# A two-layer hybrid trunk: finished tiles a stage earlier with rows in freed token space, norms and tables in fixed rounds, casts on ScalarE, the first rotation from PSUM

## Chip, core and metric

The kernel runs on one core of a Trainium2 chip. The metric is the device time of one execution in microseconds (us); before the change the median of 3 runs is 2095.43 us (2093.11 to 2095.86).

## The reference

Two layers over 2048 tokens of width 1024, each `x + y @ w_out`, then a last RMS norm. `y` joins chunked softmax attention (8 heads of 64, own chunk and 8 chunks before, a relative bias) and chunkwise retention (4 heads of 128, rotary phases, a decaying state, a norm per head), both gated with silu:

```python
hn = rms_norm(x, norm_gain)
aq, ak, av, ag, rq, rk, rv, rg = jnp.split(hn @ w_in, cuts, axis=-1)
ya = chunked_rel_attention(aq, ak, av, rel_bias)
yr = chunkwise_retention(rq, rk, rv, cos, sin)
y = jnp.concatenate([ya * silu(ag), yr * silu(rg)], axis=-1)
return x + y @ w_out
```

`rms_norm` is `x * lax.rsqrt(mean(x*x) + EPS)` times the gain. `cos` and `sin` come from `positions` times a table of inverse frequencies, and `apply_rotary` gives `[t1*c - t2*s, t1*s + t2*c]` for the two halves of a head.

## The kernel before

**Precision.** Every large product is made of three float16 products: an operand is split into a float16 upper part and a float16 remainder (`h` and `l` in the names: `hTh`/`hTl` the normed tokens, `wh`/`wl` the weights), and upper x upper, upper x remainder and remainder x upper are summed in PSUM: 24 matmuls for a contraction of 1024. Weights are first scaled by a power of two taken from their sum of squares: a square pass on ScalarE with an accumulator (`sumsq`), a cast of the sum to bfloat16 (`lowp`, on VectorE, line 316), a matmul with ones that sums over partitions (`allsum`, line 323), a few one-column operations (`norm_scale`), then the upper part on ScalarE and the remainder on VectorE (`convert`).

**Stages.** A tile is 128 tokens, a block 512 tokens (4 tiles; n = 0 to 3), a head group s = 0 to 3 is two attention heads and one retention head. For each layer l, group s and block n there are two stages. The T stage (`dense_T`, matmul line 731, output `dT`) makes queries and keys with features on the partitions, in four matmul groups j = 0 to 3 (attention query, attention key, retention query, retention key). The V stage (`dense_V`, line 752, output `dV`) makes values and gates with tokens on the partitions, in four groups a = 0 to 3, one a tile. Each group has 24 matmuls of 512 columns in 3 rounds of 8, so a stage has 12 rounds. Group sums lie in a pool of two PSUM buffers (`psD`); a buffer is free again when ScalarE and then VectorE have taken their parts from it: `v`, `gt`, `rv` on lines 760 to 763, then 766 to 770 one round later.

**Order.** The order on TensorE, ScalarE, VectorE and GpSimd is the order in which the Python code issues; only SyncE, which issues all DMAs, is ordered by a scheduler after the start. `run` drives a stage: after each round it executes what is due in a list of postponed steps (`later(k, fn)`: k rounds on), then one step of the attention of the block before, then some steps of background generators: `push(gen, steps)` queues one, and `run` deals the steps left over the rounds left (its last argument). Attention on a unit (tile a, head hx) is: scores into the one PSUM buffer `S` (lines 800, 801), bias and maximum on VectorE into a tile `sc` (line 804), exponential on ScalarE, probabilities split into `pq` (ScalarE, GpSimd), a DMA transpose to `pT`, and the product with the values (lines 820 to 822). Tiles `sc` and `pq` have two buffers each.

**Start.** The start (layer 0, group 0, block 0) is written out by hand as a list of steps. Tiles 0 to 3 are normed and transposed on TensorE; tiles 4 to 7 (`Tok`) are normed in the first V stage and turned by DMA transposes (lines 236, 237). In that first block the queries and keys of retention are copied from PSUM (`raw`, line 662), their halves are swapped by two DMAs (`swp`, lines 666, 667), and four 128x512 operations follow on VectorE (lines 670, 676). The product of keys and queries for retention's first tile (`decayed`, line 860) comes in the first attention step.

**Norms of blocks 2 and 3 and tables.** `norms_from_input` is a background generator for four tiles: load, square (ScalarE), root (VectorE, GpSimd), multiply (VectorE), upper rows (ScalarE), remainder rows (VectorE), DMA transposes. Its rows lie in the buffers of `sc` and `pq` (`row_pair`). Tables of sine and cosine for a block are 18 steps (`tables`): range reduction on VectorE, two sines on ScalarE (lines 121, 122, each change of function set a table load), eight small stores. Both run as background of the stages of the block before.

**Output projection.** Once the last group is done, `wout` goes over the 16 tiles (line 1105, `dO`). A finished row tile `y` is loaded, squared for its scale, split into rows (`rhy`, `rly`, again in the buffers of `sc` and `pq`), turned by DMA transposes into `yhy`, `yly` (`y_turn`). For the first two tiles `wout_first` does this in the last V stage (s = 3, n = 3), as background. `prep_Omax` sums the squares of `w_out` in eight pieces during the V stage of s = 2, n = 2.

## Time and profile before

| | |
|---|---|
| median of 3 runs | 2095.43 us |
| the profiled execution | 2094.75 us |
| its span on the core | 2092.8 us |
| TensorE busy / VectorE / ScalarE / GpSimd | 2004.4 / 1343.8 / 1141.3 / 432.9 us |
| mean granted TensorE clock | 0.991 |

The span runs from the first to the last instruction. A line of a timeline has the start, the length, the engine, the source line, the operation, its output and inputs by name and the count; in brackets stands the idle time before it and what ended it. A line of the waits has who waited for whom, the total, the count and the longest. Matmuls are pipelined: one that is shown with 0.38 us starts 0.22 us after the one before it at full clock.

### The profile page before, as it was taken

How to read it: one execution, taken by the hardware profiler on the slowest of the kernel's cores; microseconds unless marked ns; L12 is line 12 of the kernel's file. 1: busy time of each engine (PE TensorE's matmuls, PEld its weight loads, DVE VectorE, ACT ScalarE, POOL GpSimd, SP SyncE). 2: the span in 40 equal slices, each digit the busy share in tenths (PEclk: the TensorE clock that was granted, in tenths of full speed). 3: DMA queues.
4: the chain of work that ended last, by engine and by line, in shares of the span. 5: the costliest groups of instructions: out<-in, count | busy, mean ns of one | idle time of the engine just before them, and what ended most of it. 6: DMA issues, size and time to landing. Idle time of an engine off the chain costs nothing.

```text
span 2092.8 us, 39599 instructions
## 1 busy us (share of the span) xinstructions
PE 2004.4 (96%) x14014; PEld 1049.4 (50%) x14014; DVE 1343.8 (64%) x4031; ACT 1141.3 (55%) x2522; POOL 432.9 (21%) x509
## 2 busy tenths in 40 slices
PE   6888999999999999998999999999999999998998
PEld 4344455555555555444444555555555555554443
DVE  7676666666656666576654666666666667656643
ACT  7455665556565654455444546554655565455432
POOL 1022222222122212121000222222222222222100
PEclk9999999999999999999999999999999999999999
DMA  8767674557476764599965556655655776558874
GB/s 247 171 127 162 136 166 114 115 112 159 110 169 133 161 166 99 113 211 260 219 185 113 120 102 142 130 121 106 155 123 118 178 156 162 117 100 183 212 199 123
DMA packets 645702, 313.65 MB, mean 150 GB/s; under 512 B 459232, under 2 KB 602080, under 8 KB 645504
## 3 DMA queue, kind: packets, MB, share of 16 engines
q1 hardware_dynamic: 645504, 311.12, 66.4%
q8 instruction: 110, 1.80, 0.4%
q14 instruction: 88, 0.72, 0.1%
HBM read 123.26 MB, written 41.98 MB: 79 GB/s over the span
## 4 chain that ended last, share of the span: by engine, by line
PE 55%; DMA 7%; DVE 5%; ACT 3%; issue 1%; SPq 1%; POOL 0%; POOLq 0%; DVEq 0%; ACTq 0%
PE dT L731 18%; PE dV L752 15%; PE dO L1105 12%; DMA pT<-pq 2%; PE r L860 2%; PE S L801 2%; PE S L800 2%; PE o L820 1%; PE o L821 1%; PE o L822 1%; DVE sc L804 1%; DMA swp<-rot 1%; DMA yhy<-rhy 1%; ACT sc L807 1%; ACT pq L809 1%
## 5 line engine op out<-in xcount | busy, mean ns | idle before, releaser
L810 POOL TENSOR_TENSOR pq<-sc,pq 128x640 f16<-128x640 f32 (+4 forms) x256 | 323.8, 1265 | 1175.9 <-issue 590.7
L807 ACT ACTIVATE sc<-sc,mq,cT 128x640 f32<-128x640 f32 (+4 forms) x256 | 218.5, 853 | 558.1 <-DVE mq L806 413.7
L752 PE MATMUL dV<-whV,hTh 128*128 128x512 f16 x1024 | 354.5, 382 | 13.0 <-DVE gt L770 12.8
L731 PE MATMUL dT<-hTh,whT 128*128 128x512 f16 x1008 | 349.4, 382 | 14.7 <-DMA hTh<-hTl 9.6
L752 PE MATMUL dV<-wlV,hTh 128*128 128x512 f16 x1024 | 354.1, 381 | 0.0
L752 PE MATMUL dV<-whV,hTl 128*128 128x512 f16 x1024 | 354.0, 381 | 0.0
L731 PE MATMUL dT<-hTl,whT 128*128 128x512 f16 x1008 | 346.6, 379 | 0.0
L731 PE MATMUL dT<-hTh,wlT 128*128 128x512 f16 x1008 | 346.6, 379 | 0.0
L752 PEld LDWEIGHTS <-hTh 128*128 128x128 f16 x2048 | 197.3, 98 | 227.7 <-DVE gt L770 16.4
L731 PEld LDWEIGHTS <-whT 128*128 128x128 f16 x2016 | 192.9, 98 | 221.6 <-issue 24.1
L804 DVE CUSTOM_DVE_ANT_0 sc<-S,bias 128x640 f32<-128x640 f32 (+4 forms) x256 | 188.4, 736 | 78.8 <-PE S L801 61.1
L1105 PE MATMUL dO<-whO,yly 128*128 128x512 f16 x512 | 194.1, 379 | 2.4 <-DMA yly<-rly 2.4
L1105 PE MATMUL dO<-whO,yhy 128*128 128x512 f16 x512 | 194.0, 379 | 1.2 <-DVE gt L770 0.6
L1105 PE MATMUL dO<-wlO,yhy 128*128 128x512 f16 x512 | 194.0, 379 | 0.0
L809 ACT ACTIVATE pq<-sc 128x640 f16<-128x640 f32 (+4 forms) x256 | 171.5, 670 | 10.9 <-DMA pT<-pq 3.0
L1105 PEld LDWEIGHTS <-yhy 128*128 128x128 f16 x1024 | 99.6, 98 | 115.1 <-issue 0.8
L752 PEld LDWEIGHTS <-hTl 128*128 128x128 f16 x1024 | 99.7, 98 | 105.0 <-issue 2.8
L800 PE MATMUL S<-k,q 128*128 128x128 f16 (+3 forms) x592 | 143.1, 268 | 7.9 <-DVE mq L804 7.9
L731 PEld LDWEIGHTS <-wlT 128*128 128x128 f16 x1008 | 97.2, 98 | 101.8 <-issue 1.1
L820 PE MATMUL o<-v,pT 128*128 128x65 f16 x1120 | 129.6, 193 | 10.2 <-DMA pT<-pq 9.7
L801 PE MATMUL S<-k,q 128*128 128x128 f16 (+3 forms) x592 | 130.5, 268 | 0.0
L820 PEld LDWEIGHTS <-pT 128*128 128x128 f16 x1120 | 105.3, 97 | 49.2 <-DMA pT<-pq 21.3
(350 smaller groups left out, 3352.7 us busy)
## 6 DMA issues: line engine op xcount, KB each, us to landing
q<-qq SPq DMA_DIRECT2D x128, 128.0 KB, 2.7
yyy<-y_d SPq DMA_DIRECT2D x32, 512.0 KB, 4.6
stT<-in_w_in_dram SPq DMA_DIRECT2D x27, 512.0 KB, 4.8
stV<-in_w_in_dram SPq DMA_DIRECT2D x26, 512.0 KB, 4.5
k<-kk SPq DMA_DIRECT2D x128, 64.0 KB, 2.0
swp<-rot SPq DMA_DIRECT2D x64, 128.0 KB, 2.5
tabc<-tab SPq DMA_DIRECT2D x32, 256.0 KB, 2.7
tabs<-tab SPq DMA_DIRECT2D x32, 256.0 KB, 2.9
```

The lines of the kernel that those rows point to most:

```text
L731: pe.matmul(ps, w_[:, j, kt, :], h_[:, kt, :], start=(m == 0), stop=(m == 23))
L752: pe.matmul(ps, h_[:, kt, a * P:(a + 1) * P], w_[:, kt, :], start=(m == 0), stop=(m == 23))
L800: pe.matmul(o, st.q[:, hx, 0, cs], k_, start=True, stop=False)
L801: pe.matmul(o, st.q[:, hx, 1, cs], k_, start=False, stop=True)
L804: dve.tensor_tensor_reduce(out=v, in0=S[:, 0:w], in1=g.bias[hx][:, 640 - w:640], scale=1.0, scalar=-3.0e38, op0=ALU.add, op1=ALU.max, accu ...
L807: act.activation(v, v, AF.Exp, bias=m[:, 0:1], scale=g.c[:, 0:1])
L809: act.activation(pq[:, 0:w], v, AF.Copy)
L810: pool.tensor_tensor(pq[:, w:2 * w], v, pq[:, 0:w], op=ALU.subtract)
L820: pe.matmul(o[:, 0:65], u.p[:, b, :], v_[:, 0:65], start=(b == 0), stop=False)
L821: pe.matmul(o[:, 0:64], u.p[:, b, :], v_[:, 65:129], start=False, stop=False)
L860: pe.matmul(out_, w_, m_, start=(i == 0), stop=(i + 1 == len(pairs)))
L1105: pe.matmul(ps, h_[:, kt, :], w_[:, kt, :], start=(m == 0), stop=(m == 23))
```

## The change

- **Finished tiles.** `wout_first` runs from the T stage of s = 3, n = 3 on, a stage earlier, in 16 steps that also turn the second tile. Rows of tiles 0 to 5 (of all tiles in the last layer) and the turned forms of tiles 0 and 1 lie in spaces of normed tokens that are no longer read (`areas`, `quarter`), not in `row_pair` and not in table space.
- **Fixed rounds.** From block 1 on the first group no longer deals background steps. `slot(r, fn)` ties a step to round r, counted from the first V stage: norms of block 2 from round 18 and of block 3 from round 39, one tile every 3 rounds, loads 4 rounds ahead of the square; tables at given rounds; the weights of the next group from round 57. Rows lie in free token or start-up space, inputs in the load pool `w4` of three buffers. Block 1's T stage spans rounds 12 to 23, its V stage 24 to 35, block 2's follow from 36 and 48, block 3's from 60 and 72.
- **Casts.** `lowp` is on ScalarE, and adds two sums there where there are two.
- **First rotation.** In the first block VectorE multiplies straight from PSUM, the sine in two half-partition operations that swap the halves; the copies and swap DMAs of that block go. `decayed` for the first tile comes in the first V stage, at its 11th round.
- **Block 1's first two groups** are computed tile by tile (128 columns at a time, both groups open): 192 matmuls of 128 columns where there were 48 of 512.
- **Output-weight norms** are spread over the T and the V stage of s = 2, n = 2, with loads two pieces ahead and one reduction at the end.

```diff
-    def lowp(m1, nm):
+    def lowp(m1, nm, more=None):
         mb = b2.tile([P, 1], BF16, tag="mb", name=f"mb{nm}", bufs=4)
-        dve.tensor_copy(mb, m1)
+        if more is None:
+            act.activation(mb, m1, AF.Copy)
+        else:
+            act.activation(mb, m1, AF.Identity, bias=more[:, 0:1])
         return mb
...
+        def first_rotation(j, ps, rot):
...
+            def cosine():
+                dve.scalar_tensor_tensor(out=own, in0=ps, scalar=2.0 ** -16, in1=st.tabc, op0=ALU.mult, op1=ALU.mult)
+
+            def sine(half):
+                if half == 0:
+                    st.swp = b1.tile([P, 512], F32, tag="swp", name=f"swp{nm}_{j}")
+                i_, o_ = slice((1 - half) * 64, (2 - half) * 64), slice(half * 64, half * 64 + 64)
+                dve.scalar_tensor_tensor(out=st.swp[o_], in0=ps[i_], scalar=-2.0 ** -16, in1=st.tabs[i_], op0=ALU.mult,
+                                         op1=ALU.mult)
...
+            d = 2 * j
+            later(d, cosine)
+            later(d, lambda: sine(0))
+            later(d + 1, lambda: sine(1))
+            later(d + 2, lambda: dve.tensor_tensor(own, own, st.swp, op=ALU.add))
+            later(d + 3, lambda: act.activation(rot[:, 0], own, AF.Copy))
+            later(d + 4, lambda: dve.tensor_tensor(rot[:, 1], own, rot[:, 0], op=ALU.subtract))
...
+        parts = (l, s, n) == (0, 0, 1)
+        if parts:
+            ps, m = [None] * 2, 0
+            for (j, a) in ((0, 0), (0, 1), (0, 2), (1, 0), (1, 1), (1, 2), (0, 3), (1, 3)):
+                if a == 0:
+                    ps[j] = psD.tile([P, 512], F32, tag="dense", name=f"dT{nm}_{j}")
+                cs = slice(a * P, (a + 1) * P)
+                for i in range(24):
+                    w_, h_ = ((g.h, hh), (g.l, hh), (g.h, hl))[i // KT]
+                    pe.matmul(ps[j][:, cs], w_[:, j, i % KT, :], h_[:, i % KT, cs], start=(i == 0), stop=(i == 23))
...
+    def areas(l):
+
+        if l + 1 == DEPTH:
+            return [hT[l, i] for i in range(3)]
+        return [hT_of(l + 1, i) for i in (NS - 1, 1, 2)]
+
+    def quarter(area, i):
+        return area[i // 4].rearrange("p k c -> p (k c)")[:, i % 4 * D:(i % 4 + 1) * D]
...
-        u.rows = row_pair(u.nm)
+        if u.t < 6 or l + 1 == DEPTH:
+            i = (u.t + 2) % 6 * 2
+            u.rows = [quarter(areas(l)[2 - i // 8], (i + j) % 8 if i < 8 else 4 + (i + j) % 4) for j in range(2)]
+        else:
+            u.rows = row_pair(u.nm)
...
+            for fn in slots.pop(ring["round"], ()):
+                fn()
+            ring["round"] += 1
+            if left is None:
+                continue
...
+            for i, fn in ((-4, load), (0, sq), (1, root), (2, mul), (3, lambda: rows_hi(rows, u.x)),
+                          (4, lambda: rows_lo(rows, u.x)), (5, lambda: transpose_rows(rows, *u.h))):
+                slot(r + i, fn)
...
+    table_steps(t1, (12, 12, 13, 13, 14, 15, 17, 17))
+    table_steps(t2, [18] + list(range(22, 36)) + [36, 38, 38])
+    table_steps(t3, [36] + list(range(40, 54)) + [54, 56, 56])
+    norms_from_input(18, range(8, 12), late[0:4])
+    norms_from_input(39, range(12, 16), xs0[0:2])
+    first_prep = 57
+    for r in range(first_prep, 96):
+        for _ in range((r + 1 - first_prep) * 48 // 39 - (r - first_prep) * 48 // 39):
+            slot(r, lambda: pull(1))
+    slot(first_prep - 1, lambda: push(prep_T(0, 1, grp(0, 1)), 25))
...
+                if n == 2 and s == 2:
+                    push(prep_Omax(l, go), 23)
...
                 if n == NS - 1 and s == NSW - 1:
                     us = []
-                    push(wout_first(l, go, us), 10)
-                if n == 2 and s == 2:
-                    push(prep_Omax(l, go), 13)
+                    push(wout_first(l, go, us), 14)
+                if not first:
+                    run(dT, att, None if (l, s) == (0, 0) or (l, s, n) == (0, 1, 0) else 10 if n == 0 else 24)
```

More of the change, by code (lines that the diff above doesn't have):

```diff
@@ L693, in swap @@
                     else:
-                        later(d + 5 if first else 11, tokens)
+                        later(11, tokens)
                 if j == 2:
@@ L1150, in grp, with slot @@
         return groups[l, s]
+    slots = {}
+    ring["round"] = 0
+    def slot(r, fn):
+        slots.setdefault(r, []).append(fn)
     def run(gen, att, thirds):
@@ L1215, in hybrid_trunk, with table_steps @@
+    def table_steps(gen, rounds_):
+        for r in rounds_:
+            slot(r, lambda: next(gen, None))
     xa = b3.tile([P, 2, D], F32, tag="wh", name="xa")
```

209 lines of the change are left out of this document (111 added, 98 removed).

## The prediction

> **What bounds the kernel now.** I read the page's span first, then busy time in windows cut at the first matmul of each stage, then TensorE's waits, then the time lines round the longest of them.
>
> ```profile
> span 2092.8 us, 39599 instructions
> ```
>
> The profiled execution took 2094.75 us, 1.95 outside its span; the median shown is 0.7 above it. The columns below are the window, its length, and busy time (count) of PE, PEld, DVE, ACT and POOL, then granted clock and DMA.
>
> ```profile
> 48.39:78.91 30.52, 20.88 (x98) 9.30 (x97) 18.59 (x38) 14.56 (x31) 1.90 (x5) 0.88 0.87 195
> 78.91:103.55 24.64, 24.44 (x134) 11.84 (x135) 18.84 (x60) 12.88 (x25) 4.08 (x7) 0.94 0.52 133
> 103.55:140.13 36.58, 27.22 (x161) 12.85 (x159) 27.55 (x77) 22.29 (x50) 6.80 (x11) 0.95 0.68 129
> 140.13:166.03 25.90, 25.90 (x195) 13.82 (x196) 19.28 (x55) 13.12 (x28) 7.70 (x8) 1.00 0.64 118
> 166.03:204.90 38.87, 29.33 (x208) 15.47 (x205) 27.25 (x74) 23.10 (x48) 7.88 (x10) 0.91 0.81 177
> 204.90:236.33 31.43, 28.15 (x203) 14.51 (x204) 17.97 (x63) 18.98 (x39) 7.54 (x7) 0.95 0.69 150
> 236.33:264.20 27.87, 26.30 (x209) 14.51 (x207) 19.65 (x64) 16.50 (x40) 5.87 (x7) 1.00 0.66 128
> ...
> 599.36:627.92 28.56, 26.63 (x208) 14.36 (x206) 16.64 (x60) 20.34 (x47) 5.85 (x7) 1.00 0.87 194
> 654.09:680.23 26.14, 26.14 (x209) 14.43 (x207) 21.01 (x65) 17.20 (x41) 6.79 (x8) 1.00 0.54 114
> 859.50:893.80 34.30, 29.53 (x208) 15.32 (x206) 21.48 (x64) 19.08 (x40) 5.84 (x7) 0.90 0.68 125
> 893.80:945.00 51.20, 47.70 (x360) 25.23 (x361) 36.55 (x105) 29.25 (x54) 13.61 (x13) 1.00 0.92 215
> ...
> 1128.39:1151.17 22.78, 22.78 (x134) 11.39 (x133) 10.65 (x43) 10.81 (x27) 2.99 (x6) 1.00 0.36 84
> 1151.17:1175.72 24.55, 24.55 (x164) 12.46 (x162) 18.43 (x63) 15.88 (x41) 4.08 (x5) 1.00 0.49 119
> 1612.37:1640.74 28.37, 26.55 (x208) 14.36 (x206) 16.63 (x58) 20.22 (x47) 6.29 (x7) 1.00 0.89 197
> 1872.42:1906.64 34.22, 28.31 (x208) 15.03 (x205) 21.49 (x64) 19.08 (x40) 5.84 (x7) 0.95 0.65 138
> ```
>
> TensorE sets the time: a clean full stage is 26.14 us with TensorE never idle. Time beyond that stands in few places: block 0's V stage (30.52), block 1 (24.64 + 36.58, against 22.78 + 24.55 for the same work in layer 1: 13.9 over), block 2 (25.90 + 38.87: 12.5 over two clean stages), block 3 (31.43 + 27.87: 7.0 over), the two stages with the output-weight norms (28.56, 28.37: 4.7 over) and each layer's last V stage (34.30, 34.22: 16.2 over). These are the stages that the change edits. What TensorE waits for there:
>
> ```profile
> PE dV L752 <- DVE gt L770: 12.8, 6, 4.9
> PE dT L731 <- DMA hTh<-hTl: 9.6, 1, 9.6
> ...
> PE msT L323 <- DVE mbT L316: 3.3, 3, 1.9
> ...
> PE msV L323 <- DVE ya L832: 2.9, 2, 1.6
> ```
>
> ```profile
> 48.39 1.89 PE L752 MATMUL dV<-whV,hTh 128*128 128x512 f16 x8
> 50.11 1.89 PE L752 MATMUL dV<-whV,hTl 128*128 128x512 f16 x8
> ...
> 78.91 3.26 PE L731 MATMUL dT<-hTh,whT 128*128 128x512 f16 x8 [9.64 <-DMA hTh<-hTl]
> ...
> 192.54 0.61 PE L752 MATMUL dV<-whV,hTh 128*128 128x512 f16 x1 [4.25 <-DVE gt L770]
> ...
> 204.90 1.44 PE L731 MATMUL dT<-hTh,whT 128*128 128x512 f16 x3 [2.81 <-DMA hTh<-rhn]
> ...
> 878.17 0.27 PE L800 MATMUL S<-k,q 128*128 128x128 f16 x1 [3.28 <-DVE mq L804]
> ```
>
> The reader is to see three kinds of wait: for transposed tokens that land late (9.64, 2.81), for a PSUM buffer that ScalarE and VectorE empty late (4.25), and for attention scores that VectorE has not taken (3.28). A long one costs more than itself: the eight matmuls after 9.64 us took 3.26 us where eight take 1.89, and the three after 2.81 us took 1.44. The Trainium skill ("TensorE: Matmul & The Clock Gate", Part 1) has the clock fall to half only after about 3.4 us of idleness; by it nothing would be won back behind the waits of 2.81 and 3.28 us, and with an estimate of 2 us for each of them and for layer 1's like of the second my sum would be 6 us higher, near 2058. The 2.81 us row shows the slowing all the same, so the measurement decides and the sum stands.
>
> **Block 0's V stage, with the first rotation.** The late landing comes from SyncE's queue, where three 512 KB loads of later tiles and the swap copies stand before the last transposes:
>
> ```profile
> 70.71 0.57 SPq L1171 DMA_DIRECT2D hTh<-in_x_dram  x1
> ...
> 73.10 1.53 SPq L236 DMA_TRANSPOSE hTh<-hTl  x1
> 74.73 2.92 SPq L237 DMA_TRANSPOSE hTl<-hTl  x1
> ```
>
> Afterwards those loads go into later rounds, the four swap copies are gone, and block 1's T stage starts with tile 4 alone. That removes 9.64 and the slowing, 3.26 - 1.89: 11.0 in all. The price is on VectorE:
>
> ```profile
> 37.45 0.68 DVE L634 SCALAR_TENSOR_TENSOR qq<-dT,qq 128x512 f16<-128x512 f32 x1
> ...
> 62.77 0.28 DVE L766 SCALAR_TENSOR_TENSOR v<-dV,v 128x128 f16<-128x128 f32 x1
> ```
>
> A 512-wide operation from PSUM is 0.68. Each rotation now takes five (cosine, two half-sines, sum, remainder), and both fall in this stage: ten, 6.8 us, where four stood (2.7). So 4.1 us come in front of work such as the L766 at 62.77 that frees the buffer of the stage's fourth matmul group, which starts at 48.39 + 72 x 0.216 = 63.9. I take 3.4 us of wait and 1.7 of half speed behind it (the row at 78.91 lost 1.4, that at 878.17 is as long); 1.0 where the retention product, now inside this group, waits for the rotated keys; 0.8 in block 1, where both PSUM buffers are open at once and the third group wants the first back; and 0.4 for the smaller matmuls:
>
> ```profile
> 34.33 0.61 PE L712 MATMUL dT<-hTh,whT 128*128 128x128 f16 x8
> 34.78 0.61 PE L712 MATMUL dT<-hTl,whT 128*128 128x128 f16 x8
> ```
>
> Eight 128-wide ones start 0.45 apart, 56 ns each: 192 of them are 10.75 us, against 48 x 0.216 = 10.4. Together 7.3 is given back, **-3.7** net. Bounds: -11 if VectorE's idle time (18.59 busy of 30.52) takes it all, +2.5 if both later groups wait like that.
>
> **Blocks 1 to 3, norms and tables in fixed rounds.** Nothing is removed but the swaps; order is. The 4.25 us wait shows what order costs:
>
> ```profile
> 187.16 1.28 ACT L121 ACT_TABLE_LOAD   x1
> ...
> 189.54 1.28 ACT L761 ACT_TABLE_LOAD   x1
> ```
>
> The table's sine stands with its two table loads ahead of the gate's tanh, on the path that frees the buffer. Block 2's sine moves to the first round of a T stage, behind the last evacuation; block 3's stays in a V stage, two rounds before one. Tiles 8 to 15 get their transposes 4 and 7 rounds ahead of need (a round is 8 matmuls and a step of attention, 26.14 / 12 = 2.2 us), which clears 2.81, and their rows no longer share score buffers with attention. Casts on ScalarE stand behind the squares they follow, which clears most of 3.3 and 2.9. What stays is load: VectorE's 18.84 + 27.55 = 46.4 us in block 1, less 2.7 moved out, is 92% of the clean 47.3; block 2's 46.5 is 89% of 52.3; the clean stage at 654.09 has 80%. Above that I expect some waits to remain. Taking the slowing at 78.91 out of block 1's 13.9 leaves 12.5: **-7.5** (0 to -12.5). Block 2: **-9.5** (-4 to -12.5). Block 3: **-5.5** (-2 to -7).
>
> **Output-weight norms.** Eight squares over 24 rounds in place of 12: **-3** of 4.7 (0 to -4.7).
>
> **First two finished tiles.** In the last V stage attention's score tile waits for the transpose of the first tile's rows, which hold its buffer:
>
> ```profile
> 877.29 0.82 DVE L804 CUSTOM_DVE_ANT_0 sc<-S,bias 128x640 f32<-128x640 f32 x1 [5.11 <-DMA yhy<-rhy]
> ```
>
> The 3.28 us of TensorE and the half speed behind follow from it. Rows in freed token space cannot do that, and the two squares, casts and remainders move into the T stage before, where the output-weight work is long done. I take **-12.5** of 16.2 for both layers (-6, if the remaining waits are of other origin, to -16). In the out-projection 51.20 - 47.70 = 3.5 us is idle; rows of the next four tiles leave the score buffers too: **-1.5** (+2, if loads collide, to -3.5).
>
> **Casts at the start.** ScalarE's [128x1] operation is 0.20, VectorE's 0.15:
>
> ```profile
> 20.90 0.15 DVE L1244 CAST mbW<-m1W 128x1 bf16<-128x1 f32 x1
> ```
>
> ```profile
> 39.90 0.20 ACT L194 ACTIVATE ncT<-cT 128x1 f32<-128x1 f32 x1
> ```
>
> The first now stands behind a copy of tile 0 and comes later, the last comes sooner: 0 (-1 to +1).
>
> Sum: -3.7 - 7.5 - 9.5 - 5.5 - 3 - 12.5 - 1.5 = -43.2. 2094.75 - 43.2 = 2051.6, and 0.7 to the median: **2052**. All bounds together run from 2094.75 - 68 = 2027 to 2094.75 - 6 = 2089.
>
> **Rivals.** *VectorE is the bound in blocks 0 to 2.* For it: 92% and 89%. Against it: in the long stages it is idle 9 to 12 us itself. Then the first block gives 0, block 1 gives 0, block 2 gives 4: 2052 + 3.7 + 7.5 + 5.5 = 2069. Chance 0.20.
>
> *The finished tiles only carry their wait along:* the T stage's scores wait for ScalarE's two extra passes a tile. Against it: T stages elsewhere carry such passes without waits. 2052 + 12.5 = 2064. Chance 0.08.
>
> *Almost everything beyond clean goes:* the in-order waits all had the causes named. The best ends of blocks 1 to 3 and the last stages: 2052 - 5 - 3 - 1.5 - 3.5 - 1.7 = 2037. Chance 0.14.
>
> *Slower: the ring of three load buffers.* Tiles 8 to 15 all load into it now (four had spaces of their own), so from the fourth on each load waits for an earlier tile's release, four rounds before its squares; the finished tiles of the last stages load into it too.
>
> ```profile
> yyy<-y_d SPq DMA_DIRECT2D x32, 512.0 KB, 4.6
> ```
>
> A 512 KB load takes 4.6 us after issue. If SyncE's queue is more than four rounds behind, ScalarE stands at the square with exponentials and evacuations behind it, each time like 192.54: 4.25 and 1.7 of half speed, 6 us. Five tiles: 30, in place of some 12 of such waits that are there already. With nothing won in blocks 0 to 3 and the last stages, 2095.4 - 4.5 (norms, projection) + 30 - 12 = 2109; it decides from four held tiles on. Against it: four rounds are some 9 us. Chance 0.08. The forecast has 0.50.
>
> This measurement cannot tell 0.2%, 4 us, from no change. All cases but the ring are faster; 0.03 is for a forecast whose dear ends and a few held tiles meet near the old time: 0.89 faster, 0.03 the same, 0.08 slower. The range goes from 2031, past the third rival and near the lower bound, to 2080, past the first rival with some of the forecast's dearer ends; the ring and a little at either end lie outside.
>
> **What would show it.** Right: no wait above 1 us for token transposes at block 1's first matmul; the V stage of block 0 near 27 us with a 2 to 4 us wait for `gt`; blocks 1 and 2 at some 53 and 55 us; both last V stages under 28; no score wait on a `yhy` transpose. Wrong: `gt` waits of 4 us and more again in blocks 1 or 2 with VectorE busy throughout (first rival), ScalarE idle before a square on an `xin` load (ring of buffers), or waits for `mq` moved into the T stage before the last V stage (second).

## The result and the profile after

The changed kernel takes 2087.70 us (median of 7 runs, 2082.74 to 2091.29) against 2095.43 (2091.53 to 2095.86): a ratio of 0.9968, interval 0.9957 to 0.9979. It is faster by 0.3%, some 7 us, where 43 were forecast; 2052 and the range up to 2080 were both missed.

The page of the changed kernel, its span:

```profile
span 2085.5 us, 39797 instructions
```

Busy time in windows cut at the first matmul of each stage, in the columns of the prediction:

```profile
48.48:74.83 26.35, 22.92 (x101) 9.92 (x100) 23.21 (x47) 13.80 (x28) 2.19 (x7) 0.94 0.78 155
74.83:98.86 24.03, 23.25 (x276) 17.40 (x275) 11.96 (x41) 13.06 (x29) 3.44 (x6) 1.00 0.33 74
98.86:134.75 35.89, 27.34 (x163) 12.94 (x159) 30.24 (x83) 18.05 (x44) 6.78 (x9) 0.95 0.71 159
134.75:161.31 26.56, 26.06 (x194) 13.75 (x195) 17.23 (x52) 16.07 (x33) 7.47 (x8) 1.00 0.74 154
161.31:199.13 37.82, 30.55 (x208) 15.80 (x205) 27.08 (x74) 22.17 (x45) 8.62 (x9) 0.91 0.85 190
199.13:231.46 32.33, 28.43 (x204) 14.60 (x205) 19.52 (x62) 19.11 (x42) 7.92 (x7) 0.95 0.66 151
231.46:257.60 26.14, 26.14 (x208) 14.45 (x208) 21.77 (x72) 18.07 (x44) 5.97 (x7) 1.00 0.74 168
257.60:290.61 33.01, 28.13 (x206) 14.70 (x204) 18.01 (x63) 23.05 (x52) 8.47 (x10) 0.95 0.63 139
...
598.66:626.85 28.19, 26.64 (x210) 14.27 (x206) 18.48 (x64) 16.55 (x42) 5.84 (x7) 1.00 0.89 207
...
861.27:887.70 26.43, 26.26 (x209) 14.45 (x206) 20.22 (x58) 16.23 (x37) 5.86 (x7) 1.00 0.62 137
...
1145.72:1171.65 25.93, 25.34 (x164) 12.49 (x161) 20.54 (x65) 16.09 (x42) 4.07 (x5) 1.00 0.44 109
1612.32:1641.32 29.00, 26.93 (x208) 14.38 (x206) 18.34 (x64) 17.08 (x42) 6.53 (x7) 1.00 0.88 198
1873.07:1899.82 26.75, 26.25 (x208) 14.43 (x205) 20.20 (x58) 16.22 (x37) 5.84 (x7) 1.00 0.57 126
```

Against the rows of before, block 0's V stage (30.52 to 26.35) and the last V stages (34.30 to 26.43, 34.22 to 26.75) did what was forecast. Blocks 1 and 2 did not: their V stages went from 36.58 and 38.87 only to 35.89 and 37.82. And three places that were in no term became longer: the T stage of group 1, block 0 (27.79 to 33.01), that of group 3 in layer 0 (26.18 to 29.87), and layer 1's V stages of block 1 (24.55 to 25.93 in the row at 1145.72, and two more like it).

TensorE's waits in the changed kernel, in its time line:

```profile
66.89 0.39 PE L819 MATMUL dV<-whV,hTh 128*128 128x512 f16 x1 [2.71 <-DVE gt L837]
...
109.20 0.48 PE L867 MATMUL S<-k,q 128*128 128x384 f16 x1 [2.58 <-DVE mq L871]
...
134.75 0.59 PE L798 MATMUL dT<-hTh,whT 128*128 128x512 f16 x2 [2.98 <-DVE ya L899]
...
173.80 0.37 PE L867 MATMUL S<-k,q 128*128 128x256 f16 x1 [2.46 <-DVE mq L871]
```

The first is the price that the forecast gave the first rotation. The second and the fourth are for scores, the third stands at block 2's first matmul. For a PSUM buffer, where 4.88 and 4.25 us stood in the V stages of blocks 1 and 2 before, TensorE still waits 1.99 us (at 124.39) and 2.07 us (at 189.88). Each of these waits ends with VectorE. The late tokens went as forecast: 2.81 us at block 3's first matmul became 0.59. Why VectorE is late is in its own time line, which the prediction had not read:

```profile
102.17 0.69 DVE L720 TENSOR_TENSOR rot<-rot,tabc 128x512 f32<-128x512 f32 x1 [5.35 <-DMA tabc<-tab]
...
166.75 0.69 DVE L720 TENSOR_TENSOR rot<-rot,tabc 128x512 f32<-128x512 f32 x1 [3.57 <-DMA swp<-rot]
...
602.64 0.69 DVE L720 TENSOR_TENSOR rot<-rot,tabc 128x512 f32<-128x512 f32 x1 [6.81 <-DMA swp<-rot]
...
1617.24 0.69 DVE L720 TENSOR_TENSOR rot<-rot,tabc 128x512 f32<-128x512 f32 x1 [7.09 <-DMA swp<-rot]
```

From block 1 on, retention's queries are still rotated with the help of two swap copies, and the first product works in place on `rot`, which the copies read. It is issued three rounds after them, at the head of the V stage, and while it waits everything behind it in VectorE's queue waits too: scores, buffers, sums. The view of waits has the totals (us, times, longest), first for the kernel before, then for the changed one:

```profile
DVE rot L670 <- DMA swp<-rot: 31.7, 12, 5.5
```

```profile
DVE rot L720 <- DMA swp<-rot: 64.4, 22, 7.1
```

The wait doubled. Before, the same product stood 2.83 us in block 1 (it started at 106.95, 3.40 us into the stage) and 2.30 in block 2 (2.66 into it). In the changed kernel VectorE comes to it 2.6 us sooner in block 1, counted from the stage's start (102.17 - 5.35 - 98.86 = -2.0, against 106.95 - 2.83 - 103.55 = +0.6), and what it waits for lands no sooner (3.31 us in). What lands last there is the row of the table, as the profile names it. In the first group the change also issues the loads of the table three rounds later (`later(3, tab_load)`), which its list above does not say, and so they stand behind the copies, the second of which went out at 98.71:

```profile
99.34 0.58 SPq L627 DMA_DIRECT2D tabc<-tab  x1
```

With the 2.6 us that the copies take in block 2 (below) they would have held the product until about 101.3, an estimate; so some 4.5 of the 5.35 us would stand without the table. In block 2 the copies themselves are late. SyncE's queue there:

```profile
160.43 1.39 SPq L236 DMA_TRANSPOSE hTh<-xa  x1
162.26 1.23 SPq L237 DMA_TRANSPOSE hTl<-xa  x1
163.67 0.48 SPq L716 DMA_DIRECT2D swp<-rot  x1
164.19 0.60 SPq L717 DMA_DIRECT2D swp<-rot  x1
```

ScalarE had `rot` ready at 158.54 + 0.57 = 159.1; the copies go out 4.6 us later, behind two token transposes that the fixed rounds put there, and the product starts 2.6 us after the second one's issue.

Layer 1 shows the same in small. Before, SyncE issued the copies ahead of a store of `yr`; in the changed kernel the scheduler put that store first:

```profile
1146.05 0.47 SPq L666 DMA_DIRECT2D swp<-rot  x1
1146.57 0.59 SPq L667 DMA_DIRECT2D swp<-rot  x1
1147.20 0.58 SPq L927 DMA_DIRECT2D y_d<-yr  x1
```

```profile
1140.54 0.46 SPq L992 DMA_DIRECT2D y_d<-yr  x1
1141.22 0.48 SPq L716 DMA_DIRECT2D swp<-rot  x1
1141.75 0.60 SPq L717 DMA_DIRECT2D swp<-rot  x1
```

VectorE then stands 3.27 us until 1145.73, 4.0 us after the second copy was issued, and the V stage has 25.93 in place of 24.55.

### The profile page after: what moved, and what is told of

Same layout as the page of the kernel before. It is cut to its first block, busy times and chain, and to the rows that moved or that the text cites. A ratio compares the mean times of both kernels' runs of the same rounds, so it can differ in the third digit from the quotient of the medians.

```text
span 2085.5 us, 39797 instructions
## 1 busy us (share of the span) xinstructions
PE 2010.4 (96%) x14158; PEld 1059.1 (51%) x14158; DVE 1337.2 (64%) x3950; ACT 1149.5 (55%) x2576; POOL 433.8 (21%) x509
## 5 line engine op out<-in xcount | busy, mean ns | idle before, releaser
L798 PE MATMUL dT<-hTh,whT 128*128 128x512 f16 x992 | 343.0, 380 | 4.4 <-DVE ya L899 3.0
L1194 PE MATMUL dO<-whO,yly 128*128 128x512 f16 x448 | 170.4, 380 | 2.0 <-DMA yly<-rly 1.6
L1194 PE MATMUL dO<-wlO,yhy 128*128 128x512 f16 x448 | 170.6, 381 | 0.0
L1194 PE MATMUL dO<-whO,yhy 128*128 128x512 f16 x448 | 170.4, 380 | 0.0
L867 PE MATMUL S<-k,q 128*128 128x128 f16 (+3 forms) x592 | 143.5, 269 | 6.4 <-DVE mq L871 6.4
L798 PEld LDWEIGHTS <-wlT 128*128 128x128 f16 x992 | 96.0, 98 | 101.3 <-issue 2.5
L1194 PEld LDWEIGHTS <-yhy 128*128 128x128 f16 x896 | 87.6, 98 | 101.6 <-issue 1.6
L933 DVE SCALAR_TENSOR_TENSOR sh<-sh,state 128x128 f16<-128x128 f16 x120 | 94.7, 789 | 64.3 <-ACT sh L929 64.1
```

The costliest lines, as they stand in the source:

```text
L798: pe.matmul(ps, w_[:, j, kt, :], h_[:, kt, :], start=(m == 0), stop=(m == 23))
L867: pe.matmul(o, st.q[:, hx, 0, cs], k_, start=True, stop=False)
L933: dve.scalar_tensor_tensor(out=dst[:, 1], in0=dst[:, 0], scalar=-2.0 ** 11, in1=src, op0=ALU.mult, op1=ALU.add)
L1194: pe.matmul(ps, h_[:, kt, :], w_[:, kt, :], start=(m == 0), stop=(m == 23))
```

## The experiments

Ratios are to the kernel before on the same chip. The whole change has 0.9968 in them. "Held" names the theory that VectorE stands at the rotation's first product and all behind it comes late, "load" the rival of the prediction that VectorE simply has too much to do.

**e1_tiles: the finished tiles alone.** The kernel before with `wout_first`, `areas`, `quarter`, `y_turn` and the calls of the change:

```diff
+                if n == NS - 1 and s == NSW - 1:
+                    us = []
+                    push(wout_first(l, go, us), 14)
...
-                if n == NS - 1 and s == NSW - 1:
-                    us = []
-                    push(wout_first(l, go, us), 10)
```

> The kernel before with the finished-tiles part of the change alone (wout_first a stage earlier, rows and turned forms in freed token space, in the projection too). If this part gives what the changed kernel's last V stages show (34.30 to 26.43 and 34.22 to 26.75, together 15.3 us) and costs nothing elsewhere: 2080 us, the last V stages near 26.5, so that alone it beats the whole change and the rest of the change costs some 7 us. If part of the gain needs the other edits (casts, spread norms) or the projection pays for it: 2086 or more, with waits in the T stage before or in the projection that the changed kernel does not have.

2083.84 us, 0.9943 (0.9931 to 0.9954); last V stages 27.84 and 28.36 us. This part alone gives 12 us and beats the whole change. The rest of the change, added to it, costs time.

**e2_rot: the rotation's products later in group 0 of layer 0.**

```diff
-                    d = 3
+                    hold = (l, s) == (0, 0)
+                    d = 5 if hold and j == 2 else 3
                     later(d, turned(raw, raw, st.tabc, ALU.mult))
+                    if hold:
+                        d -= 1
                     later(d + 1, turned(swp, swp, st.tabs, ALU.mult))
...
-                    later(2, swap)
+                    later(3 if (l, s) == (0, 0) else 2, swap)
```

> The changed kernel; in layer 0's first group the query rotation's products are issued two rounds later (the sine product in the same round as the cosine product), and the key's swap copies one round later. Same instructions. Theory 'held': in blocks 1 and 2 VectorE stands 5.35 and 3.57 us at the first product of the rotation until the table rows and swap copies land, and all that is queued behind it comes late; then the V stage of block 1 falls from 35.9 to 29 to 31 us, that of block 2 from 37.8 to 32 to 34, the whole by 8 to 12 us to some 2077. Theory 'load' (VectorE has too much work in these stages): the two stages stay within 1.5 us of 35.9 and 37.8, and the whole within 3 us of 2087.7.

2086.05 us, 0.9955 (0.9943 to 0.9967). Windows of block 1's V stage and of block 2:

```profile
98.70:130.31 31.61, 25.42 (x161) 12.47 (x159) 30.02 (x79) 18.28 (x44) 6.79 (x9) 0.98 0.83 182
130.31:159.01 28.70, 28.70 (x194) 14.70 (x195) 17.13 (x51) 15.84 (x33) 7.48 (x8) 0.90 0.74 141
159.01:194.62 35.61, 27.26 (x207) 14.28 (x205) 28.23 (x74) 22.17 (x45) 8.16 (x9) 1.00 0.95 202
```

The V stages fall by 4.3 and 2.2 us, with VectorE's busy time nearly the same in block 1 (30.24 and 30.02) and larger in block 2 (27.08 and 28.23). Held is right on the mechanism, too hopeful on block 2; the T stage between them gives 2.1 back, at a granted clock of 0.90. Of the 8 to 12 us that held expected for the whole, the interval shows nothing that can be told from the change's own ratio.

**e3_bare: no transfer to wait for in blocks 1 and 2.** `swp` is made from `raw` by the sine product, the copies go, and the table loaded is block 0's:

```diff
+                    if bare:
+                        later(d, turned(swp, raw, st.tabs, ALU.mult))
+                        later(d + 1, turned(raw, raw, st.tabc, ALU.mult))
```

> The changed kernel with blocks 1 and 2 of layer 0's first group rotated without the swap copies and with block 0's table, loaded early (the output is then not the reference's): VectorE's instructions are the same in number and size, but none of them waits for a transfer there. Theory 'held': V stages of blocks 1 and 2 at 28 to 31 and 30 to 33 us, no wait of TensorE above 1.5 us for scores there, the whole 10 to 14 us shorter. Theory 'load': unchanged within 1.5 us a stage.

2077.86 us, 0.9919 (0.9906 to 0.9932), 10 us under the changed kernel:

```profile
97.98:128.78 30.80, 25.32 (x162) 12.56 (x160) 28.56 (x78) 17.96 (x44) 6.80 (x9) 0.99 0.77 167
156.39:191.64 35.25, 29.21 (x208) 15.06 (x205) 28.06 (x74) 22.18 (x45) 8.64 (x9) 0.95 0.82 181
```

Block 1's stage falls by 5.1, as held has it; block 2's by 2.6, less than held expected.

**e4_less: less work for VectorE.** The range reduction of two tables is left out:

```diff
+            if n < 2:
+                dve.scalar_tensor_tensor(out=dst, in0=kk, scalar=-c, in1=dst, op0=ALU.mult, op1=ALU.add)
```

> The changed kernel without the range reduction of the tables of blocks 2 and 3 (15 VectorE operations of 0.28 to 0.43 us for each table, some 5.4 us; their other steps, sines and stores stay; the output is then not the reference's). About 4 us of it lie in block 1's V stage, 2.5 in block 2's. Theory 'load': these stages shrink by as much or more, 4 to 6 and 2.5 to 4 us. Theory 'held': VectorE still stands at the rotation's first product, only the catching up is shorter: 1 to 2 us and 0 to 1 us.

2089.41 us, 0.9978 (0.9965 to 0.9990): no gain.

```profile
99.73:134.07 34.34, 25.75 (x162) 12.62 (x160) 26.01 (x71) 18.34 (x44) 6.57 (x9) 1.00 0.74 166
160.28:197.49 37.21, 28.79 (x207) 14.89 (x205) 23.87 (x64) 22.18 (x45) 8.62 (x9) 0.95 0.86 195
```

VectorE has 4.2 and 3.2 us less to do (30.24 to 26.01, 27.08 to 23.87), and the stages shorten by 1.5 and 0.6. While VectorE stands, its load is not the bound. Without the stand it comes next in block 1's V stage: there VectorE is busy for 30.02 of 31.61 us in e2_rot and for 28.56 of 30.80 in e3_bare, 95 and 93%. No run takes work from VectorE alone with the stand gone.

**e5_prep: the weights of group 1 three rounds sooner.**

```diff
-    for r in range(first_prep, 96):
-        for _ in range((r + 1 - first_prep) * 48 // 39 - (r - first_prep) * 48 // 39):
+    for r in range(first_prep, 93):
+        for _ in range((r + 1 - first_prep) * 48 // 36 - (r - first_prep) * 48 // 36):
```

> The changed kernel; the 48 background steps that prepare the second group's weights are dealt over 36 rounds from round 57 on instead of 39, so that they end three rounds earlier. Theory 'late weights' (the fixed rounds put the end of this preparation three rounds later than before, and TensorE waits for its last norm, 2.65 us, and for the upper part of the last weights, 2.24 us): the T stage of group 1, block 0 falls from 33.0 to 27.8 to 29 us, block 3's stages before it grow by at most 1, the whole by 4 to 5 us to some 2083. Rival: that stage is long for another reason (ScalarE stands at the bias tile); then it stays above 31.5 and the whole within 2 us of 2087.7.

2089.81 us, 0.9973 (0.9962 to 0.9984). Block 3's V stage, then the two stages of group 1, block 0:

```profile
231.63:263.88 32.25, 29.17 (x210) 15.55 (x207) 24.56 (x75) 18.66 (x43) 5.83 (x7) 0.89 0.49 107
263.88:290.45 26.57, 26.57 (x205) 14.09 (x203) 13.95 (x54) 20.12 (x48) 6.99 (x8) 1.00 0.82 181
290.45:320.96 30.51, 27.90 (x202) 14.86 (x201) 22.13 (x62) 16.52 (x39) 7.07 (x10) 0.94 0.67 146
```

The T stage loses its excess (33.01 to 26.57) and its neighbours take it (26.14 to 32.25, 25.91 to 30.51): TensorE waits 3.08 us for a cast in block 3's V stage instead. In the code a norm's matmul comes a set number of these steps behind the cast that it needs; more steps a round leave it less time.

**e6_casts: casts on VectorE again.**

```diff
-        if more is None:
-            act.activation(mb, m1, AF.Copy)
-        else:
-            act.activation(mb, m1, AF.Identity, bias=more[:, 0:1])
+        dve.tensor_copy(mb, m1)
```

> The changed kernel with the casts of the weight norms (and the additions of their two sums) on VectorE again. Theory 'late casts' (on ScalarE they stand behind exponentials and evacuations, and what follows from the norm is late in every group): the three V stages of block 1 in layer 1 go from 25.7 to 25.9 back to 24.55 us, the T stages of block 0 of the later groups (29.87, 27.65) back to 26.2, the whole shrinks by 5 to 8 us to 2080 to 2083, though block 3's first T stage may grow by up to 1.5. My forecast's reason (casts there clear waits): the whole grows by 2 to 4 us. Rival: no effect, within 2 us.

2088.19 us, 0.9958 (0.9946 to 0.9971). Layer 1's V stages of block 1 go back to 24.55, 24.54 and 24.97, and the stages round group 1's start in layer 0 grow by 2.2, 1.6 and 2.6 us. In layer 1 the swap copies are again issued ahead of the store, and VectorE no longer stands in that stage.

**e7_omax: output-weight norms in the V stage again.**

```diff
-                if n == 2 and s == 2:
-                    push(prep_Omax(l, go), 23)
...
+                if n == 2 and s == 2:
+                    push(prep_Omax(l, go), 13)
```

> The changed kernel with the output-weight norms in the V stage alone, as before the change. If spreading them gave the 3 us in all that I forecast: the T and V stage together longer by 1.5 in each layer. If it only moved the loss (T stage 25.90 to 27.05, V stage 28.56 to 28.18 in layer 0; 25.89 to 26.06 and 28.37 to 29.01 in layer 1): T stages back to 25.9, V stages 28.3 to 28.6, the whole shorter by 1 to 2 us.

2087.87 us, 0.9962 (0.9948 to 0.9975). T stages 25.90 and 25.89, V stages 28.87 and 28.40: 109.06 for the four, against 110.29 in the changed kernel and 108.72 before. The spreading gave nothing there.

**e8_spread: norms and tables sooner, on top of e2_rot.**

```diff
-    table_steps(t2, [18] + list(range(22, 36)) + [36, 38, 38])
-    table_steps(t3, [36] + list(range(40, 54)) + [54, 56, 56])
-    norms_from_input(18, range(8, 12), late[0:4])
-    norms_from_input(39, range(12, 16), xs0[0:2])
+    table_steps(t2, [16] + list(range(18, 32)) + [36, 38, 38])
+    table_steps(t3, [33] + list(range(36, 50)) + [60, 61, 61])
+    norms_from_input(16, range(8, 12), late[0:4])
+    norms_from_input(35, range(12, 16), xs0[0:2])
```

> The kernel with the later rotation (e2_rot), and on top of it norms and tables of blocks 2 and 3 started 2 to 4 rounds earlier, so that less of them lies in the V stages: block 2's norms from round 16 (was 18), block 3's from 35 (was 39), table steps of block 2 in rounds 18 to 31 (was 22 to 35), of block 3 in 36 to 49 (was 40 to 53), its two sines in round 60, ahead of no tanh. Theory 'work in the V stages' (with the transfer wait gone, the V stages of blocks 1 and 2 are still 31.6 and 35.6 us because VectorE and ScalarE hand norms to and fro there, while both have half of block 1's T stage idle): 29 to 30 and 30 to 32, the T stages longer by at most 2 each, the whole 4 to 7 us under e2_rot, some 2080. Rival: the V stages' handoffs are attention's own and the norms only fill gaps: both within 1.5 us of 31.6 and 35.6.

2084.26 us, 0.9934 (0.9922 to 0.9947). V stages of blocks 1 and 2: 28.01 and 33.96; but block 3's T stage grew from 33.03 to 34.87, and block 0's V stage, where VectorE now stands 1.89 us at a table row, from 26.42 to 28.54. Norms and tables do lengthen the stage they lie in.

**e9_first: the first rotation alone.** The kernel before with `first_rotation`, block 1 by parts and `decayed` in the V stage.

```diff
+                if first:
+                    first_rotation(j, ps, rot)
+                    return
...
-                if (n, s) == (0, 0) and not first:
+                if (n, s) == (0, 0):
                     later(11, lambda n=n, g=g, st=st: decayed(l, s, n, g, st, 0))
```

> The kernel before with the first rotation from PSUM, decayed in the first V stage and block 1's first two groups tile by tile, and nothing else of the change. My forecast for this part was -3.7 us, and the changed kernel's block 0 V stage (30.52 to 26.35) and block 1 T stage (24.64 to 24.04) show -4.8. If the part stands alone: block 0's V stage 26 to 27, the whole 4 to 5 us shorter, 2090 to 2091 against some 2095. If it only works with the late loads moved into later rounds (their three 512 KB loads stay here ahead of the last transposes): V stage 29 or more, the whole within 2 us of before.

2091.27 us, 0.9977 (0.9967 to 0.9986), 5 us; stages 26.36 and 23.80. It stands alone.

**e10_rotall: the later rotation everywhere.** As e2_rot, with `hold = True`.

> The changed kernel with the later rotation (as in e2_rot) in all stages of both layers. Theory 'held' everywhere: where VectorE stood longest at the rotation's first product (6.81 us in layer 0's and 7.09 in layer 1's V stage of group 2, block 2; 4.01 and 4.35 in the last V stages), the stage loses its excess: 28.2 and 29.0 to 26.5 to 27.5; the whole 3 to 5 us under e2_rot. Rival: outside the first group those stands are covered by TensorE's own work: within 1.5 us of e2_rot.

2066.03 us, 0.9853 (0.9839 to 0.9866): 22 us under the changed kernel by the medians, several times the expectation. V stages of blocks 1 and 2, the T stage of group 1, then V stages of both layers:

```profile
99.64:131.13 31.49, 26.59 (x162) 12.76 (x160) 29.97 (x79) 18.20 (x44) 6.79 (x9) 0.95 0.84 182
157.54:193.10 35.56, 28.89 (x207) 15.11 (x205) 28.18 (x74) 22.17 (x45) 8.15 (x9) 0.95 0.94 203
249.44:283.26 33.82, 29.26 (x205) 14.93 (x203) 17.72 (x66) 23.61 (x54) 8.47 (x10) 0.90 0.62 137
590.40:617.11 26.71, 26.30 (x209) 14.35 (x206) 17.69 (x59) 16.65 (x42) 6.18 (x7) 1.00 0.95 221
848.38:874.48 26.10, 26.10 (x208) 14.41 (x206) 20.45 (x55) 16.11 (x37) 6.18 (x7) 1.00 0.67 149
1130.81:1155.36 24.55, 24.55 (x164) 12.49 (x162) 19.71 (x61) 15.31 (x42) 4.08 (x5) 1.00 0.46 115
1591.29:1617.85 26.56, 26.29 (x208) 14.35 (x206) 18.03 (x60) 17.32 (x45) 6.72 (x8) 1.00 1.01 208
```

The stages with the output-weight norms lose their excess, the last V stage is clean, and layer 1's V stage of block 1 is back at 24.55 with the casts still on ScalarE. SyncE still issues the store of `yr` there ahead of the copies (1125.63, then 1126.32 and 1126.85); with the product two rounds later this does no harm.

VectorE's stand has not gone, though:

```profile
DVE rot L720 <- DMA swp<-rot: 29.5, 12, 5.8
```

```profile
594.46 0.69 DVE L720 TENSOR_TENSOR rot<-rot,tabc 128x512 f32<-128x512 f32 x1 [5.79 <-DMA swp<-rot]
```

It is gone in blocks 1 to 3 of the first group, which give 8.9 of the 24.6 us between the spans of the two profiles. In all it is about what the kernel before had (31.7), and the V stage of group 2, block 2 keeps 5.79 of its 6.81 us and is short all the same. There the edit changed what stands behind the product in VectorE's queue (attention's `ya` and a product of retention now go ahead of it), and it also moved the key's copies and its transpose in SyncE's queue. Which of these gives the rest was not separated.

**c1_mix** joined that with casts on VectorE, the old output-weight norms, norms as in e8_spread, and

```diff
-    table_steps(t3, [36] + list(range(40, 54)) + [54, 56, 56])
+    table_steps(t3, [32] + list(range(33, 47)) + [47, 49, 49])
...
-    first_prep = 57
+    first_prep = 51
```

**c2_mix** is built up from the kernel before: the edits of e1_tiles, e9_first and e10_rotall, and nothing else.

> A mix from the runs so far: the changed kernel with the later rotation in all stages, casts on VectorE, output-weight norms in the V stage as before, norms from rounds 16 and 35, table steps of block 3 in rounds 33 to 46 with its sines in round 47 (in a T stage) and stores in 49, and the second group's preparation from round 51 on, at about one step a round. If the parts add (e8_spread's 12 us under before, 4 from the casts in layer 1, 1 from the norms, and 4 to 5 at group 1's first stages, since the preparation is no longer dealt at more than one step a round): some 2072 to 2077 against 2095. If the time beyond clean in the first group is work that only moves between stages: no better than e8_spread, 2083 to 2086.

> A mix built up from the kernel before: finished tiles a stage sooner, the first rotation from PSUM with block 1 by parts, and the later rotation in all stages; norms, tables, casts and output-weight norms as before the change. If the parts add (11 to 12 for the tiles, 4 to 5 for the first rotation, 3 to 5 for the later rotation): 2075 to 2078 against 2095. If the background's order gives blocks 1 and 2 the same length whatever is issued later: 2080 to 2084.

2074.13 us, 0.9883 (0.9866 to 0.9899), and 2073.18 us, 0.9886 (0.9873 to 0.9900). In c1_mix block 1's V stage is 27.91, but block 2's 40.26: TensorE waits 5.44 us there for a norm of the preparation that starts sooner. Both stay behind e10_rotall, which keeps all parts of the change. In c2_mix the V stages of blocks 1 and 2 have 36.14 and 37.09 us although VectorE waits for no copy and no table row in them: with norms and tables dealt as before the change, something else holds them, and the fixed rounds with the later product have 31.49 and 35.56.

**e11_before_rot: the later rotation without the change.** The edit of e2_rot on the kernel before, with `hold` in all stages but block 0 and the last V stages.

> The kernel before with the later rotation in all stages but the last V stage of each layer (there its buffers are taken over by the finished tiles) and block 0. If VectorE's stand grew with the change (before it, casts and additions kept VectorE late, so that the swap copies had landed when it came to the rotation): 5 to 8 us under before, some 2088 to 2091 against 2096. If it cost the kernel before as much as the changed one: 18 to 24 us, 2072 to 2078.

2095.77 us, 1.0005 (0.9996 to 1.0014): nothing. Blocks 1 and 2's V stages fall by 2.0 and 2.6, and 1.3, 3.5 and 1.6 are lost again in group 1's first V stages and the projection. VectorE's wait falls from 31.7 to 19.4 us, and nothing comes of it. The same edit, with the last V stages as well (1.0 us there), gives 1.15% on the changed kernel. The expectation's reason, casts and additions that kept VectorE late, has no run of its own.

**e12_rot_casts, e13_rot_omax: parts taken back from e10_rotall.** The edits of e6_casts and of e7_omax on it.

> The later rotation in all stages (e10_rotall, 2066) with the casts of the weight norms on VectorE again. If casts on ScalarE help once VectorE no longer stands: 2068 to 2071. If they are late on ScalarE whatever VectorE does: 2060 to 2064. If it does not matter: 2066 within 2 us.

> The later rotation in all stages (e10_rotall, 2066) with the output-weight norms in the V stage alone, as before the change. If spreading them does what I forecast (3 us for both layers) once VectorE no longer stands: V stages of group 2, block 2 from 26.7 and 26.6 back to 28.3 to 28.8, T stages unchanged, the whole 2 to 4 us longer, 2068 to 2070. If the later rotation alone made these stages short: 26.6 to 27 and no difference above 1 us.

2070.90 us, 0.9881 (0.9867 to 0.9894), and 2073.51 us, 0.9897 (0.9882 to 0.9912). Now both parts pay, though for the casts the two intervals only just part (0.9867 and 0.9866): without the spread norms the V stages are 29.25 and 28.80 again instead of 26.71 and 26.56; with the casts on VectorE the T stage of group 3, block 0 has 29.88 for 26.90 and that of group 1 35.30 for 33.82. The 7 us between the medians of e13_rot_omax and e10_rotall are more than these stages hold (4.5 with their T stages); in its one profile block 3's first T stage is 2.8 longer, for which there is no test.

**e14_rot_spread, e15_bias, e16_prep: on from e10_rotall.** Norms and tables sooner as in c1_mix; then ScalarE's scaling of the bias tiles two rounds behind GpSimd's memsets; then the preparation two rounds ahead at the same density:

```diff
-            act.activation(bt, bt, AF.Copy, scale=g.ci[:, 0:1])
+                later(2, lambda bt=bt: act.activation(bt, bt, AF.Copy, scale=g.ci[:, 0:1]))
...
-    first_prep = 57
-    for r in range(first_prep, 96):
+    first_prep = 55
+    for r in range(first_prep, 94):
```

> The later rotation in all stages (e10_rotall, 2066) with norms of blocks 2 and 3 from rounds 16 and 35, table steps of block 2 in rounds 18 to 31, of block 3 in 33 to 46, its sines in round 47 and stores in 49; the second group's preparation stays at round 57. If the V stages of blocks 1 and 2 (31.5 and 35.6) are long because norms and tables share VectorE and ScalarE with attention there: 28 and 31 to 33, T stages 1 to 3 longer together, the whole 3 to 6 us shorter, 2060 to 2063. If the work only moves: 2065 to 2068.

> e14_rot_spread (2063) with ScalarE's scaling of the bias tiles issued two rounds after GpSimd's memsets instead of right behind them. If ScalarE's stand there holds the T stages of block 0: that of group 1 falls from 33.6 to 30 to 31.5, those of the other groups (26.8 to 28.1) by about 1, the whole 3 to 6 us shorter, 2057 to 2060. If the late end of the weights' preparation holds it: 33 or more there, the whole within 2 us of 2063.

> e15_bias with the second group's preparation two rounds earlier at the same density (rounds 55 to 93). If the late end holds the T stage of group 1: TensorE's wait for the upper part of the last weights goes, the stage falls by 2 to 4 us against e15_bias and blocks 2 and 3 grow by at most 1: 2055 to 2060. If the steps collide with the norms in block 2's V stage: that stage grows by as much, the whole unchanged within 2 us of e15_bias.

2062.91 us, 0.9844 (0.9827 to 0.9861); 2061.52, 0.9832 (0.9819 to 0.9846); 2060.89, 0.9823 (0.9810 to 0.9837). Each step lies inside the interval of the one before; all three together are below e10_rotall's. V stages of blocks 1 and 2 fall to 27.78 and 32.22 in the first; group 1's T stage goes 33.57, 32.15, 30.28, but the V stage behind it rises from 25.92 to 28.67 and 27.59. TensorE waits for the weights at that stage's first matmul, which the windows count to the T stage, and the V stage loses what the matmuls behind the wait run slower (granted clock 0.90 and 0.94). The wait is 4.97 us in e15_bias and in the last kernel still

```profile
274.59 1.01 PE L825 MATMUL dV<-whV,hTh 128*128 128x512 f16 x2 [3.13 <-ACT whV L334]
```

This last kernel is the best one measured, 1.8% under the kernel before.

## Why the prediction was wrong, step by step

Stage times of before, of the changed kernel and of e10_rotall; forecast and measured are changes against before.

| step of the forecast | forecast | before | after | measured | e10_rotall |
|---|---|---|---|---|---|
| first rotation (block 0 V, block 1 T) | -3.7 | 55.16 | 50.38 | -4.8 | -4.3 |
| block 1 (V) | -7.5 | 36.58 | 35.89 | -0.7 | -5.1 |
| block 2 | -9.5 | 64.77 | 64.38 | -0.4 | -2.8 |
| block 3 | -5.5 | 59.30 | 58.47 | -0.8 | -3.0 |
| output-weight norms, T and V, both layers | -3 | 108.72 | 110.29 | +1.6 | -3.4 |
| last V stages | -12.5 | 68.52 | 53.18 | -15.3 | -16.3 |
| out-projection, layer 0 | -1.5 | 192.96 | 193.60 | +0.6 | -1.0 |
| group 1, block 0 | none | 54.64 | 58.92 | +4.3 | +5.1 |
| group 3, block 0, T, layer 0 | none | 26.18 | 29.87 | +3.7 | +0.7 |
| block 1 V stages of groups 0 to 2, layer 1 | none | 73.63 | 77.49 | +3.9 | 0 |

**The step that failed is "Blocks 1 to 3, norms and tables in fixed rounds", with 22.5 of the 43.2 us; it measured 1.9.** It said that "nothing is removed but the swaps; order is", and that above VectorE's load "some waits" would remain. The swaps that went were block 0's; the copies of all other blocks stayed, and so did the product that waits for them three rounds later, in place, at the head of VectorE's queue. The prediction put down TensorE's waits to what TensorE waited for (tokens, `gt`) and did not read VectorE's own: 31.7 us for swap copies stood in the view of waits of the kernel before. In the changed kernel this wait took the place of the old causes. e3_bare and e2_rot show it in blocks 1 and 2 (5.1 and 2.6 us; 4.3 and 2.2).

The second fault of that step is its load. It set VectorE's work against both stages of block 1 together (92% of 47.3). The fixed rounds put 30.24 us of it into the V stage, which has 24.55 when clean, and 11.96 into the T stage; so the V stage could hardly become clean, however the waits went. e14_rot_spread, with norms and tables sooner, has 26.32 us of VectorE there in a stage of 27.78.

The stand is not the whole of the missing 20.6 us either. With the later product blocks 1 to 3 gain 10.9 of the 22.5 (e10_rotall), and 14.9 with norms and tables sooner (e14_rot_spread, which loses 1.0 in block 1's T stage).

**It is an interplay, not a sum.** The later rotation alone gives nothing (1.0005), the change alone 0.3%, both together 1.5%. e1_tiles and e9_first give 12 and 5 us alone, more than the whole change: its remaining parts (fixed rounds, casts, spread norms) cost some 10 us as they stand, if parts add, and gain once the product comes later (e10_rotall against c2_mix, which lacks them: 0.9853 to 0.9886).

**What was right.** The first rotation (2.71 us of wait for `gt` where 2 to 4 were named; no wait for tokens at block 1's first matmul), the last V stages (under 28, no score waiting for a transpose; somewhat more than forecast), and with the later product the output-weight norms (-3.4 for -3; e13_rot_omax shows that it takes their spreading). The projection's -1.0 for -1.5 proves little: it takes 191.6 to 194.3 us in runs on the changed kernel that do not edit it.

**What was left out of the sum.** The preparation of group 1's weights ends later against attention's units: TensorE waits 2.65 us for its last norm and 2.24 for the upper part of the last weights, +4.3 in group 1, block 0, and ScalarE stands 1.97 at a bias tile. e5_prep, e15_bias and e16_prep moved this loss about and removed part of it. In group 3's T stage (+3.7) TensorE waits 1.97 us for a transpose, with slower matmuls behind; the stage has 27.1 to 30.4 us in runs that edit nothing there (e5_prep, e2_rot), so its cause is open. The forecast gave casts on ScalarE "most of 3.3 and 2.9" us of waits for weight norms; they stayed (msT and msV: 2.4 and 2.6 us after). And SyncE's order moved in layer 1, where no edit was costed at all.

**The rivals.** "VectorE is the bound" named the place, and 2069, but its mechanism is not what held the changed kernel (e4_less); with the stand gone it is the next bound in block 1. The finished tiles did not carry their wait along (last T stage 26.08 us, as before). The ring of load buffers did not hold: no wait of ScalarE for an `xin` load is in the trace.

**Still open.** In e3_bare, where nothing in it waits for copies or tables, block 2's V stage has 35.25 us, 9 over clean, with VectorE busy for 28.06. Moving norms and tables out takes it to 32.2 to 34.0; what the rest is was not settled. Nor is it shown why the stand cost the kernel before nothing.

## What to carry to other kernels

Read the waits of every in-order engine, not only of the one that sets the time. An instruction that waits for a transfer at the head of a queue can cost nothing in one kernel and be the bound in the next, once the causes ahead of it are cleared. Its total does not tell: of 31.7 us in the kernel before nothing could be won, of 64.4 in the changed one 1.15% of the time, and with that won 29.5 us are still there. What tells is a run with the instruction issued later; give it its distance in rounds from the transfer's issue, and look at what the transfer's own queue issues ahead of it. Here two rounds more were worth over three times the change. Set an engine's load against each stage by itself, not against a pair. Where parts that are good alone sum to less than the best of them, look for one shared wait before undoing any of them.

## What the runs showed of the hardware that was not expected

- TensorE's matmuls ran at half pace behind waits shorter than the 2.81 us of the prediction. In the changed kernel's time line the rows after a wait of 1.97 us for a transpose have 512-column matmuls 0.43 us apart, then 0.22 again:

```profile
695.98 0.20 PE L887 MATMUL o<-v,pT 128*128 128x65 f16 x1 [1.97 <-DMA pT<-pq]
...
698.25 0.63 PE L798 MATMUL dT<-hTh,whT 128*128 128x512 f16 x1
698.68 0.63 PE L798 MATMUL dT<-hTh,wlT 128*128 128x512 f16 x1
...
699.50 0.38 PE L798 MATMUL dT<-hTh,whT 128*128 128x512 f16 x1
699.72 0.38 PE L798 MATMUL dT<-hTh,wlT 128*128 128x512 f16 x1
```

- After 1.99 us at 124.39 the matmuls ran 0.22 apart at once: the length of a wait alone does not say whether the pace halves. The Trainium skill ("TensorE: Matmul & The Clock Gate", Part 1) has the clock fall after about 3.4 us of idleness; the row at 695.98 shows the half pace behind 1.97.
- The same pair of copies took 2.6 us (block 2) and 4.0 us (layer 1) from the second one's issue to the product that waits for them. What makes the difference is not shown: in layer 1 a store stands right ahead of the pair.
